# Layer 0 of a hybrid backbone: the context tokens' output projection and MLP made inside the attention stage

## The chip, the cores and the metric
One Trainium2 chip, one core of it. The metric is the device time of one launch in microseconds (us). The kernel before takes 4530.56 us, the median of three runs (4529.67 to 4532.49).

## The reference
Two layers act on 1024 latent tokens and 256 context tokens with 1024 channels. A layer normalises, projects into four head groups (gated DeltaNet, Hyena, HGRN2, differential attention), joins them, applies one output projection with a gated residual, then a squared-ReLU MLP with a gated residual. The last layer returns the latent tokens alone, so only layer 0 (and not layer 1) needs the context's output projection and MLP.

```python
def diff_attn_mixer(p_lat, p_ctx, ...):   # latent queries see context and latent keys
    ...                                   # context queries see context keys alone
# each layer, for both streams (the last layer: latent alone)
x = x + g1 * (concat(mixers) @ w_out)
h = modulate(x, ln2_w, shift2, scale2)
x = x + g2 * (square(relu(h @ mlp_w1)) @ mlp_w2)
```

## The kernel before, in words
Tokens lie along the free dimension: columns 0 to 1023 are latent, 1024 to 1279 context. Products of weights run three times, with operands split into a high and a low float32r part (`mm3`: wh·xh, wh·xl, wl·xh). `weight` loads a piece of a weight matrix of 128x512 into one of three `wraw` buffers through SP's DMA queue, ScalarE rounds it (`whi`), and GpSimd subtracts (`wlo`).

The instruction order is what the Python generators emit, then placed by a scheduler on each engine. `mix(lead, fill, ratio)` takes a lead generator and, after each step of weight w, as much of the fill as comes to ratio·w; what is left of the fill is drained at the end. `weave` does this between two fills. The attention stage (`mix(at[0], fill, RD[l])`) has `attn` as lead. Its fill (`rest`) is what is left of `hyena`, with the modulation products `mods` of this layer woven in, then `mods` of the next layer.

`attn` goes over four heads. Each has ten tiles of 128 queries: eight latent (1280 keys), then two context (256 keys). A tile is `scores` (the `psc` matmuls, a VectorE maximum, a ScalarE exponential, twice), `weights` (VectorE), `turn` (ten `ptr` transposes through PSUM, ScalarE copies), and per two tiles `values` (`pav`, `prb`); after a head, `norm` (`pss`). PSUM in this stage: two score tiles of three banks each, and two banks called `big`, which rotate among `ptr`, `pav`, `prb`, `pss`, hyena's and `mods`' tiles (`nbig` = 2, and `m` falls back on `big` when `nm` = 0).

`tail` comes after the attention stage, alone. It loads the mixers' outputs `o`, splits them, and goes over w_out (8 row blocks), then 8 MLP blocks of mlp_w1 (4 row blocks each) and mlp_w2 (8 each). With every weight piece loaded it makes three chunks of columns (512, 512, 256) in layer 0, two in layer 1, with five `big` banks. A chunk's 12 or 24 matmuls accumulate in one bank (`pt`); `residual` (VectorE, tile `tx`) or `hidden` (ScalarE Relu, VectorE square, split) empties it. Its last w_out pass, first mlp_w1 pass and last mlp_w2 pass go chunk by chunk and load their weights again.

Of the kernel before, what the change touches and what calls it, by code (L numbers as in the profile page):

```python
# [30 lines left out]
RC, RD, RM = [1.0, 1.0], [1.1, 0.8], [0.8, 0.8]  # L31
# [209 lines left out]
class K:  # L241


    def __init__(self, tc, ins, outs, dbg=None, upto=None):
        self.tc, self.nc, self.i, self.o = tc, tc.nc, ins, outs
        self.dbg, self.upto = dbg, upto
        self.done = set()
        self.pending = None

# [902 lines left out]
    def attn(self, l, qp):  # L1152
# [8 lines left out]
        def load(i, b):  # L1161

            out = ops[i, b] = []
            for j in range(2):
                for nm, n in (("q", 128 * NQ), ("k", T)):
                    t = pools[heads.index((i, b)) % 2].tile([128, T], F32R, tag=f"{nm}{j}", name=f"{nm}{j}")[:, :n]
                    c0 = 64 * b + 32 * j
                    nc.sync.dma_start(t.bitcast(F32), S["d" + nm, i][c0:c0 + 32, :, :n].rearrange("c r t -> (c r) t"))
                    out.append(t)

        pools = [qp]
        load(*heads[0])
# [21 lines left out]
        def scores(i, b, qi):  # L1194

            Q, Kt = ops[i, b][0::2], ops[i, b][1::2]
# [56 lines left out]
        def norm(i, b, oT):  # L1253
            tn = 64 * NQ
            o = S["o", 6 + i][64 * b:64 * b + 64, :128 * NQ].rearrange("e (q y t) -> y e q t", y=2, t=128)
            for a in range(0, tn, 320):
                e = min(tn, a + 320)
                sq = tp.tile([128, 320], F32, tag="sq", name="sq", bufs=1)[:, :e - a]
                r = tp.tile([128, 320], F32, tag="r", name="r", bufs=1)[:, :e - a]
                nc.scalar.activation(sq, oT[:, a:e], AF.Square)  # L1260
                p = self.m("pss")
                nc.tensor.matmul(p[:, :e - a], self.c["bones64"], sq, start=True, stop=True)
                self.rsqrt(r, p[:, :e - a], sq, 1.0 / 64, 64 * EPS)
                nc.vector.scalar_tensor_tensor(oT[:, a:e], oT[:, a:e], sw, r, ALU.mult, ALU.mult)
            for y in range(2):
                nc.gpsimd.dma_start(o[y], oT[64 * y:64 * y + 64, :tn].rearrange("e (q t) -> e q t", t=128))
# [3 lines left out]
        for h, (i, b) in enumerate(heads):  # L1270
            for qi in range(NQ):
                if qi == 2 and h + 1 < len(heads):
                    load(*heads[h + 1])
                cur = scores(i, b, qi)
# [3 lines left out]
                if qi == 0:  # L1278
                    old, oT = oT, tp.tile([128, 64 * NT], F32, tag="oT", name="oT")

                def todo(i=i, b=b, qi=qi, cur=cur, oT=oT):
# [8 lines left out]
                    if qi == NQ - 1:  # L1290
                        norm(i, b, oT)
# [280 lines left out]
    def tail(self, l, xp):  # L1572

        nc, tc, S = self.nc, self.tc, self.S
        full = l < DEPTH - 1
        toks = T if full else SEQ
        chunks = [(a, n) for a, n in CHUNKS if a < toks]
        M = self.Ms[l]
        nch = len(chunks)
        with ExitStack() as es:  # L1580
            hp = es.enter_context(tc.tile_pool(name=f"th{l}", bufs=1, side="right", reuse_waits="tile"))
            self.wp = es.enter_context(tc.tile_pool(name=f"tw{l}", bufs=2, side="right", reuse_waits="tile"))
            tp = es.enter_context(tc.tile_pool(name=f"tt{l}", bufs=4, reuse_waits="tile"))
            self.ps = self.fs = es.enter_context(tc.tile_pool(name=f"psT{l}", bufs=1, space=PSUM, reuse_waits="tile"))
            self.nbig, self.nm, self.nw, self.ww, self.lo_eng = 5, 3, 4, 512, nc.gpsimd

            def tmp(name, n):
                return tp.tile([128, 512], F32, tag="raw", name=name)[:, :n]

            def tiles(name):  # L1590

                return [[[hp.tile([128, n], F32R, tag=f"{y}{k}{a}", name=f"{name}{y}{k}")
                          for k in range(KT)] for a, n in chunks] for y in "hl"]
            oh, ol = tiles("o")
            for ks in (range(6), (6, 7)):
                for c, (a, n) in enumerate(chunks):
                    for k in ks:
                        raw = tmp("o", n)
                        nc.sync.dma_start(raw, S["o", k][:, a:a + n])
                        self.split(oh[c][k], ol[c][k], raw, lo_eng=nc.vector if k % 2 else nc.gpsimd)  # L1600
            x = []
            for k in range(KT):
                t = xp.tile([128, T], F32, tag=f"x{k}", name=f"tx{k}")
                nc.sync.dma_start(t[:, :toks], self.X[k][:, :toks])  # L1604
                x.append(t)
            rs = [xp.tile([128, n], F32, tag=f"r{a}", name=f"r{a}") for a, n in chunks]

            def product(wt, xh, xl, nk, done, cs):
                for c in cs:
                    a, n = chunks[c]  # L1610
                    p = self.big("pt")[:, :n]
                    for k in range(nk):
                        wh, wl = wt[k // 4]
                        sl = slice(128 * (k % 4), 128 * (k % 4) + 128)
                        self.mm3(p, wh[:, sl], wl[:, sl], xh[c][k], xl[c][k], k == 0, k == nk - 1)
                    done(p, c, a, n)

            def residual(m, G, norm=False, out=False):
                def done(p, c, a, n):
                    v = 0 if a < SEQ else 1  # L1620
                    xm = x[m][:, a:a + n]
                    nc.vector.scalar_tensor_tensor(xm, p, G[:, m, v:v + 1], xm, ALU.mult, ALU.add)  # L1622
                    if norm:
                        self.norm_sum(rs[c], xm, m, tmp("sq", n))
                        if m == KT - 1:
                            self.norm_factor(rs[c], rs[c], tmp("s4", n))
                    if out:
                        nc.sync.dma_start(out[m][:, a:a + n], xm)
                return done
            hh, hl = tiles("h")  # L1630
            for cs in ((0,), range(1, nch)):
                for m in range(KT):
                    product(self.weight(self.i["w_out"][l, m]), oh, ol, KT, residual(m, M["G1"], True), cs)
                for c in cs:
                    a, n = chunks[c]
                    v = 0 if a < SEQ else 1
                    for k in range(KT):
                        self.norm_apply(tmp("t", n), x[k][:, a:a + n], M["A2"][:, k, v:v + 1], M["B2"][:, k, v:v + 1], rs[c],
                                        hh[c][k], hl[c][k])
            if self.upto == "out":  # L1640
                return self.dump("x", lambda d: [nc.sync.dma_start(d[k], x[k]) for k in range(KT)]), rs
            if full:
                self.X = [self.dram(f"x{k}_{l}", [128, T]) for k in range(KT)]
                out = self.X
            else:
                out = self.o["yT"]
            with tc.tile_pool(name=f"tf{l}", bufs=1, reuse_waits="tile") as fp:
                for blk in range(8):
                    fh, fl = [[[fp.tile([128, n], F32R, tag=f"{y}{j}{a}", name=f"f{y}{j}") for j in range(4)]
                               for a, n in chunks] for y in "hl"]  # L1650

                    def hidden(j):
                        def done(p, c, a, n):
                            f = tmp("f", n)
                            nc.scalar.activation(f, p, AF.Relu)  # L1655
                            nc.vector.tensor_mul(f, f, f)  # L1656
                            self.split(fh[c][j], fl[c][j], f)
                        return done

                    for cs in (((0,), range(1, nch)) if blk == 0 else (range(nch),)):  # L1660
                        for j in range(4):
                            product(self.weight(self.i["mlp_w1"][l, 4 * blk + j]), hh, hl, KT, hidden(j), cs)
                    last = blk == 7
                    for cs in ([(c,) for c in range(nch)] if last else (range(nch),)):
                        for m in range(KT):
# [228 lines left out]
```

## Time and profile before

| what | value |
|---|---|
| median of three runs | 4530.56 us |
| the profiled execution, its own time | 4536.95 us |
| its span | 4535.1 us |
| mean granted TensorE clock | 0.932 of full speed |
| busy share of the span: TensorE, VectorE, ScalarE, GpSimd | 90%, 51%, 36%, 24% |

TensorE's share is high over the whole span, but it is an average over stages. In the page's 40 slices (113 us each) slices 11 to 14, in which layer 0's attention stage lies, show TensorE at 7 to 9 tenths with VectorE at 7 to 8, and slices 15 to 21 (layer 0's tail) TensorE at 9 tenths or more with VectorE at 2. A stage's end is set by the engine whose queue is fullest there and by who waits for whom.

### The profile page before, as it was taken

Reading aid. Unit: us, or ns where it says so; the run is one execution under the profiler, and the core shown is the slowest. Engines: PE = TensorE matmul, PEld = TensorE weight load, DVE = VectorE, ACT = ScalarE, POOL = GpSimd, SP = SyncE. Lnnn points to the kernel's source line nnn. Section 1 sums busy time; section 2 is a strip of 40 time slices with the busy share of each in tenths; the row PEclk is TensorE's granted clock in tenths of the full one; section 3 lists DMA queues with packets and bytes.
Section 4 is the critical chain, followed back from the end, with each engine's and each line's share of the span. In section 5 each row is a group of like instructions: output and inputs, shape, how many; then the busy total and the mean of one; then the engine's idle time right before and its main releaser. Section 6 shows DMA issues by size and latency. Waiting matters only on the chain. (4 is left out here: it accounts for less than half of the span.)

```text
span 4535.1 us, 81524 instructions
## 1 busy us (share of the span) xinstructions
PE 4064.8 (90%) x33312; PEld 3296.7 (73%) x33312; DVE 2330.6 (51%) x4579; ACT 1617.4 (36%) x3165; POOL 1075.7 (24%) x1101
## 2 busy tenths in 40 slices
PE   6998799887778799999999887999877789999999
PEld 3787677665555688888888766777655567888887
DVE  5856455766887452222222657556567875222222
ACT  4544512442445441111112554514324464212222
POOL 0234022000211343333333121121001215433333
PEclk8999899987889899999999998899877889999999
DMA  5335743335323421111112336534342233111112
GB/s 180 103 116 159 189 126 123 103 122 186 119 82 136 147 70 38 40 38 40 38 38 70 98 89 170 177 109 141 123 169 104 68 130 126 61 49 49 49 49 89
DMA packets 387434, 466.48 MB, mean 103 GB/s; under 512 B 137683, under 2 KB 246355, under 8 KB 385140
## 3 DMA queue, kind: packets, MB, share of 16 engines
q1 hardware_dynamic: 385236, 456.28, 31.2%
q8 instruction: 263, 4.31, 0.4%
q0 software_dynamic: 1824, 4.98, 0.4%
q14 instruction: 111, 0.91, 0.1%
HBM read 341.71 MB, written 119.44 MB: 102 GB/s over the span
## 5 line engine op out<-in xcount | busy, mean ns | idle before, releaser
L255 POOL TENSOR_TENSOR wlo<-wraw,whi 128x512 fp32r<-128x512 f32 x360 | 478.8, 1336 | 737.7 <-ACT whi L254 735.5
L254 ACT CAST whi<-wraw 128x512 fp32r<-128x512 f32 (+1 forms) x480 | 296.4, 620 | 910.5 <-PE pt L260 752.4
L1622 DVE SCALAR_TENSOR_TENSOR tx<-pt,mod,tx 128x512 f32<-128x512 f32 (+1 forms) x360 | 250.9, 697 | 589.9 <-PE pt L261 588.9
L261 PE MATMUL pt<-hh,wlo 128*128 128x512 f32 (+1 forms) x1280 | 471.7, 368 | 2.8 <-POOL wlo L255 2.8
L260 PE MATMUL pt<-fl,whi 128*128 128x512 f32 (+1 forms) x1280 | 472.5, 369 | 0.0
L260 PE MATMUL pt<-hl,whi 128*128 128x512 f32 (+1 forms) x1280 | 472.4, 369 | 0.0
L259 PE MATMUL pt<-hh,whi 128*128 128x512 f32 (+1 forms) x1280 | 471.7, 369 | 0.4 <-ACT f L1655 0.4
L259 PE MATMUL pt<-fh,whi 128*128 128x512 f32 (+1 forms) x1280 | 471.7, 369 | 0.0
L261 PE MATMUL pt<-fh,wlo 128*128 128x512 f32 (+1 forms) x1280 | 471.7, 369 | 0.0
L1656 DVE TENSOR_TENSOR f<-f 128x512 f32<-128x512 f32 (+1 forms) x160 | 149.5, 936 | 622.7 <-ACT f L1655 616.9
L259 PE MATMUL pproj<-hh,whi 128*128 128x512 f32 (+1 forms) x960 | 372.4, 388 | 10.9 <-ACT u L500 10.7
L260 PE MATMUL pproj<-hl,whi 128*128 128x512 f32 (+1 forms) x960 | 362.7, 378 | 0.0
L261 PE MATMUL pproj<-hh,wlo 128*128 128x512 f32 (+1 forms) x960 | 360.2, 375 | 0.0
L255 POOL TENSOR_TENSOR fl<-f,fh 128x512 fp32r<-128x512 f32 (+1 forms) x160 | 191.5, 1198 | 390.3 <-ACT fh L254 390.3
L261 PEld LDWEIGHTS pt<-hh,wlo 128*128 128x128 f32 x1280 | 241.4, 189 | 44.2 <-POOL wlo L255 4.0
L259 PEld LDWEIGHTS pt<-hh,whi 128*128 128x128 f32 x1280 | 241.5, 189 | 40.9 <-ACT f L1655 0.8
L259 PEld LDWEIGHTS pt<-fh,whi 128*128 128x128 f32 x1280 | 241.5, 189 | 40.9 <-ACT whi L254 0.2
L261 PEld LDWEIGHTS pt<-fh,wlo 128*128 128x128 f32 x1280 | 241.3, 189 | 40.6 <-issue 0.5
L260 PEld LDWEIGHTS pt<-fl,whi 128*128 128x128 f32 x1280 | 241.5, 189 | 40.3 <-POOL fl L255 0.3
L260 PEld LDWEIGHTS pt<-hl,whi 128*128 128x128 f32 x1280 | 241.5, 189 | 40.1 <-issue 0.2
L529 PE MATMUL pproj<-whi,hh 128*128 128x256 f32 (+2 forms) x624 | 193.0, 311 | 35.9 <-ACT whi L254 21.7
L259 PEld LDWEIGHTS pproj<-hh,whi 128*128 128x128 f32 x960 | 187.1, 195 | 51.3 <-ACT u L500 12.9
(376 smaller groups left out, 8292.6 us busy)
## 6 DMA issues: line engine op xcount, KB each, us to landing
wraw<-mlp_w SPq DMA_DIRECT2D x296, 256.0 KB
modw<-mod_w SPq DMA_DIRECT2D x80, 512.0 KB
wraw<-w_cm SPq DMA_DIRECT2D x88, 256.0 KB
wraw<-w_out SPq DMA_DIRECT2D x64, 256.0 KB
kv<-kvd SPq DMA_DIRECT2D x40, 256.0 KB
k<-dk SPq DMA_DIRECT2D x16, 640.0 KB
modw<-mod_w SPq DMA_DIRECT2D x4, 2048.0 KB
ksl<-X SPq DMA_DIRECT2D x16, 512.0 KB
```

The source lines that it names most:

```text
L254: (hi_eng or nc.scalar.copy)(hi, src)
L255: (lo_eng or nc.gpsimd).tensor_tensor(lo, src, hi.bitcast(F32), ALU.subtract)
L259: nc.tensor.matmul(ps, wh, xh, start=start, stop=False)
L260: nc.tensor.matmul(ps, wh, xl, start=False, stop=False)
L261: nc.tensor.matmul(ps, wl, xh, start=False, stop=stop)
L529: nc.tensor.matmul(p[:, :w - c0], hh[k][:, sl], wh[:, b + c0:b + w], start=first, stop=False)
L1622: nc.vector.scalar_tensor_tensor(xm, p, G[:, m, v:v + 1], xm, ALU.mult, ALU.add)
L1656: nc.vector.tensor_mul(f, f, f)
```

## The change
In layer 0, `attn` takes the context queries of all four heads first (two tiles each, with their own loads of q and k), then the latent queries of all four. `tail` becomes a generator that takes its chunks, its pools and its output as arguments. `tail_context` runs it for the context's 256 columns; it follows hyena in the attention stage's fill, with the next layer's `mods` woven in at 0.3, and the stage's ratio `RD[0]` goes from 1.1 to 1.6. The context's result goes to DRAM (`Xn`, and the norm's factor `Rn`). The tail after the attention stage makes the two latent chunks, and takes the context's columns of x and its factor back from DRAM. Layer 1 has the same work as before (its `norm` goes by 256 columns in place of 320).

```diff
-RC, RD, RM = [1.0, 1.0], [1.1, 0.8], [0.8, 0.8]
+RC, RD, RM = [1.0, 1.0], [1.6, 0.8], [0.8, 0.8]
...
     def attn(self, l, qp):
-        NQ = NT if full else NLT
+        seq = [(i, b, range(*r)) for r in ([(NLT, NT)] if full else []) + [(0, NLT)] for i in range(2) for b in range(2)]
...
-                for nm, n in (("q", 128 * NQ), ("k", T)):
+                for nm, r in (("q", slice(128 * qs[0], 128 * qs[-1] + 128)), ("k", slice(0 if lat else SEQ, T))):
...
-            for a in range(0, tn, 320):
-                e = min(tn, a + 320)
+            for a in range(t0, tn, 256):
+                e = min(tn, a + 256)
...
-        for h, (i, b) in enumerate(heads):
-            for qi in range(NQ):
-                if qi == 2 and h + 1 < len(heads):
-                    load(*heads[h + 1])
-                cur = scores(i, b, qi)
+        for s, (i, b, qs) in enumerate(seq):
+            for qi in qs:
+                if qi - qs[0] == (2 if len(qs) > 2 else 0) and s + 1 < len(seq):
+                    load(s + 1)
+                cur = scores(s, qi)
...
-    def tail(self, l, xp):
+    def tail(self, l, xp, es, chunks, side, out, store=None):
...
+        yield x, rs
...
             def product(wt, xh, xl, nk, done, cs):
...
+                yield n / 512 * nk / KT
...
+        if store is not None:
+            nc.sync.dma_start(store, rs[0])
+
+    def tail_context(self, l):
+        assert self.ctx_out
+        with ExitStack() as es:
+            xp = es.enter_context(self.tc.tile_pool(name=f"txc{l}", bufs=1, side="right", reuse_waits="tile"))
+            g = self.tail(l, xp, es, CHUNKS[2:], "right", self.Xn, self.Rn)
+            next(g)
+            yield from g
...
                             yield from weave(self.hyena(l), m2, RM[l])
                             if full:
-                                yield from self.mods(l + 1, range(16), mp)
+                                self.Xn = [self.dram(f"x{k}_{l}", [128, T]) for k in range(KT)]
+                                self.Rn = self.dram(f"r_{l}", [128, CTX])
+                                yield from weave(self.tail_context(l), self.mods(l + 1, range(16), mp), 0.3)
...
-                xs, rs1 = self.tail(l, xp)
+                    g = self.tail(l, xp, ts, LCHUNKS, "left", self.Xn if full else self.o["yT"])
+                    xs, rs1 = next(g)
+                    if full:
+                        for k in range(KT):
+                            nc.sync.dma_start(xs[k][:, SEQ:], self.Xn[k][:, SEQ:])
+                        nc.sync.dma_start(rs1[2], self.Rn)
+                    run(g)
```

TensorE, between two latent tiles of the attention stage after hyena has ended (`ptr` transposes, `psc` scores, `pmod` modulation, `pt` tail products). Before:

```order
L1230 MATMUL ptr<-c_ident,p_15100 128x128 x10
L368 MATMUL pmod<-modw,cst 32x128 x8
L354 MATMUL pmodT<-c_sel,modr 128x2 x4
L1230 MATMUL ptr<-c_ident,p_15186 128x128 x8
L1208 MATMUL psc<-k_14524,q_14522 128x512
L1230 MATMUL ptr<-c_ident,p_15186 128x128 x2
L1208 MATMUL psc<-k_14524,q_14522 128x512
L1242 MATMUL pav<-wT,vt 64x128 x20
L1248 MATMUL prb<-c_ident,rb 128x128
```

And with the change, where 48 `pt` matmuls follow the last row shown:

```order
L369 MATMUL pmod<-modw,cst 32x128 x8
L1234 MATMUL ptr<-c_ident,p_15099 128x128 x4
L1212 MATMUL psc<-k_14354,q_14352 128x256
L1234 MATMUL ptr<-c_ident,p_15099 128x128 x6
L1246 MATMUL pav<-wT,vt 64x128 x20
L1252 MATMUL prb<-c_ident,rb 128x128
L1212 MATMUL psc<-k_14358,q_14356 128x512 x2
L1212 MATMUL psc<-k_14358,q_14356 128x256
L1212 MATMUL psc<-k_14354,q_14352 128x512
L260 MATMUL pt<-hh_14705,whi 128x256
```

Groups of 24 to 96 context products now stand between the tiles' own matmuls; all 1728 lie between the first score and the tail, 1296 of them ahead of the last head's `pss`, 432 behind it.

SP's DMA queue, where the context's part ends and the tail after it begins (`tx_14...` is the context's x, `tx_19...` the x of the tail, `x_0_...` DRAM):

```order
L1637 DMA x_0_14625<-tx_14700 128x256
L1873 DMA tx_19250<-x_0_14624 128x256
L1637 DMA x_0_14626<-tx_14702 128x256
L1873 DMA tx_19252<-x_0_14625 128x256
L1873 DMA tx_19254<-x_0_14626 128x256
L1671 DMA r_14627<-r_14704 128x256
L271 DMA wraw<-w_out 128x512 x3
L1874 DMA r_19258<-r_14627 128x256
L1606 DMA o<-o_0_123 128x512
```

The tail's first weights stand behind the context's last stores and their loads back.

## Rows read from the trace of the kernel before

**Rows 1.** Busy time by stretch: us from span's start, length, each engine, clock, DMA share, GB/s.

```profile
core 0: us, PE busy (x) PEld busy (x) DVE busy (x) ACT busy (x) POOL busy (x), PEclk, DMA share, GB/s
1125.00:1385.00 260.00, 186.41 (x1314) 144.99 (x1314) 213.37 (x275) 107.86 (x202) 47.34 (x52) 0.83 0.28 99
1385.00:1497.00 112.00, 90.22 (x1005) 65.17 (x1003) 78.34 (x136) 65.90 (x134) 11.39 (x22) 0.92 0.43 147
1125.00:1497.00 372.00, 276.63 (x2316) 210.16 (x2316) 291.71 (x410) 173.76 (x335) 58.73 (x74) 0.86 0.32 114
1497.00:1600.00 103.00, 85.75 (x369) 68.00 (x369) 45.35 (x59) 41.77 (x74) 45.79 (x36) 0.88 0.45 151
1497.00:2528.00 1031.00, 1009.14 (x5197) 862.28 (x5196) 314.91 (x427) 268.41 (x487) 361.38 (x290) 0.99 0.19 61
3727.00:4535.00 808.00, 792.60 (x3460) 651.96 (x3460) 226.07 (x270) 212.61 (x354) 321.11 (x246) 0.99 0.21 70
```

**Rows 2.** Timeline of TensorE: start, us, instruction; in layer 0's tail, then in attention.

```profile
1700.72 0.28 PE L259 MATMUL pt<-fh,whi 128*128 128x256 f32 x1
1700.84 0.28 PE L260 MATMUL pt<-fl,whi 128*128 128x256 f32 x1
1700.96 0.28 PE L261 MATMUL pt<-fh,wlo 128*128 128x256 f32 x1
...
1702.04 0.40 PE L260 MATMUL pt<-fl,whi 128*128 128x512 f32 x1
1702.27 0.39 PE L261 MATMUL pt<-fh,wlo 128*128 128x512 f32 x1
...
1452.82 0.71 PE L1230 MATMUL ptr<-c_ident,p 128*128 128x128 f32 x5
```

**Rows 3.** Groups by form in layer 0's tail (1500:2530): count, busy us, mean ns, idle before.

```profile
L255 POOL TENSOR_TENSOR wlo<-wraw,whi 128x512 fp32r<-128x512 f32 x180 | 241.3, 1349 | 411.1 <-ACT whi L254 410.2 <-issue 0.3
L254 ACT CAST whi<-wraw 128x512 fp32r<-128x512 f32 x180 | 111.0, 618 | 394.7 <-PE pt L260 380.5 <-DMA wraw<-w_out 6.2 <-issue 5.6
L261 PE MATMUL pt<-fh,wlo 128*128 128x256 f32 x256 | 72.9, 285 | 0.0
L1656 DVE TENSOR_TENSOR f<-f 128x256 f32<-128x256 f32 x32 | 37.9, 1185 | 74.6 <-ACT f L1655 72.6 <-POOL fl L255 2.1
L1622 DVE SCALAR_TENSOR_TENSOR tx<-pt,mod,tx 128x256 f32<-128x256 f32 x72 | 34.7, 483 | 46.0 <-PE pt L261 46.0
L255 POOL TENSOR_TENSOR fl<-f,fh 128x256 fp32r<-128x256 f32 x32 | 23.5, 736 | 0.0
```

**Rows 4.** Groups by form, attention after hyena's end (1385:1497).

```profile
L1209 DVE TENSOR_REDUCE mx<-psc 128x1 f32<-128x1280 f32 x23 | 34.2, 1485 | 3.9 <-PE psc L1208 3.8
L1210 ACT ACTIVATE p<-psc,mx 128x1280 f32<-128x1280 f32 x23 | 30.6, 1331 | 14.2 <-DVE mx L1209 11.3 <-DVE mod L355 1.5 <-DVE sm L1217 1.2
L1230 PE MATMUL ptr<-c_ident,p 128*128 128x128 f32 x144 | 25.2, 308 | 4.7 <-DVE modr L376 1.7 <-ACT wT L1232 1.4 <-DVE mod L355 0.8
L1220 DVE SCALAR_TENSOR_TENSOR p<-p,sm,p 128x1280 f32<-128x1280 f32 x12 | 18.6, 1549 | 0.4
L1232 ACT COPY wT<-ptr 128x512 f32<-128x512 f32 x28 | 15.5, 588 | 18.3 <-PE ptr L1230 18.3
L1209 DVE TENSOR_REDUCE mx<-psc 128x1 f32<-128x256 f32 x8 | 3.4, 420 | 0.9 <-PE psc L1208 0.8
```

**Rows 5.** Groups by form, attention with hyena beside it (1125:1385).

```profile
L1230 PE MATMUL ptr<-c_ident,p 128*128 128x128 f32 x192 | 33.0, 307 | 13.9 <-DVE sm L1217 5.2 <-DVE u L1563 2.2 <-DVE p L1220 2.2
L1557 PE MATMUL py<-bil,X 128*128 128x256 f32 x128 | 39.0, 472 | 16.2 <-DVE X L1546 11.4 <-issue 4.7
```

**Rows 6.** Who waited for whom in 1385:1497: us in total, times, longest.

```profile
PEld psc L1208 <- ACT p L1210: 13.1, 13, 4.2
...
PEld ptr L1230 <- ACT wT L1232: 4.5, 12, 1.1
...
PEld pmod L368 <- ACT wT L1232: 3.9, 9, 1.0
```

More of the change, by code (lines that the diff above doesn't have):

```diff
@@ L1569, in hyena @@
         es.close()
-    def tail(self, l, xp):
+    def tail(self, l, xp, es, chunks, side, out, store=None):
         nc, tc, S = self.nc, self.tc, self.S
-        full = l < DEPTH - 1
-        toks = T if full else SEQ
-        chunks = [(a, n) for a, n in CHUNKS if a < toks]
+        t0, t1 = chunks[0][0], sum(chunks[-1])
+        wide = chunks[0][1]
         M = self.Ms[l]
         nch = len(chunks)
-        with ExitStack() as es:
[L1581 to L1665, printed above, removed]
-                            product(self.weight(self.i["mlp_w2"][l, blk, m], 512, 1), fh, fl, 4,
-                                    residual(m, M["G2"], last and full, last and out), cs)
-        return x, rs
@@ new lines, in tail, with tmp, tiles @@
+        pool = lambda name, bufs, side: es.enter_context(
+            tc.tile_pool(name=f"{name}{side[0]}{l}", bufs=bufs, side=side, reuse_waits="tile"))
+        full = l < DEPTH - 1
+        hp = pool("th", 1, "right")
+        self.wp = pool("tw", 2, "right")
+        self.nw, self.ww, self.lo_eng = 4, 512, nc.gpsimd
+        tp = pool("tt", 4, side)
+        def tmp(name, n):
+            return tp.tile([128, wide], F32, tag="raw", name=name)[:, :n]
+        def tiles(name):
+            return [[[hp.tile([128, n], F32R, tag=f"{y}{k}{a}", name=f"{name}{y}{k}")
+                      for k in range(KT)] for a, n in chunks] for y in "hl"]
@@ new lines, in tail @@
+        oh, ol = tiles("o")
+        for ks in (range(6), (6, 7)):
+            for c, (a, n) in enumerate(chunks):
+                for k in ks:
+                    raw = tmp("o", n)
+                    nc.sync.dma_start(raw, S["o", k][:, a:a + n])
+                    self.split(oh[c][k], ol[c][k], raw, lo_eng=nc.vector if k % 2 else nc.gpsimd)
+        x = []
+        for k in range(KT):
+            t = xp.tile([128, T if side == "left" else t1 - t0], F32, tag=f"x{k}", name=f"tx{k}")
+            nc.sync.dma_start(t[:, :t1 - t0], self.X[k][:, t0:t1])
+            x.append(t)
@@ new lines, in tail, with product @@
+        rs = [xp.tile([128, n], F32, tag=f"r{a}", name=f"r{a}") for a, n in (CHUNKS if full and side == "left" else chunks)]
+        yield x, rs
+        def product(wt, xh, xl, nk, done, cs):
+            for c in cs:
+                a, n = chunks[c]
+                p = self.big("pt")[:, :n]
+                for k in range(nk):
+                    wh, wl = wt[k // 4]
+                    sl = slice(128 * (k % 4), 128 * (k % 4) + 128)
+                    self.mm3(p, wh[:, sl], wl[:, sl], xh[c][k], xl[c][k], k == 0, k == nk - 1)
+                done(p, c, a, n)
+                yield n / 512 * nk / KT
@@ new lines, in tail @@
+        hh, hl = tiles("h")
+        for cs in ((0,), range(1, nch)):
+            for m in range(KT if cs else 0):
+                yield from product(self.weight(self.i["w_out"][l, m]), oh, ol, KT, residual(m, M["G1"], True), cs)
+            for c in cs:
+                a, n = chunks[c]
+                v = 0 if a < SEQ else 1
+                for k in range(KT):
+                    self.norm_apply(tmp("t", n), x[k][:, a - t0:a - t0 + n], M["A2"][:, k, v:v + 1], M["B2"][:, k, v:v + 1],
+                                    rs[c], hh[c][k], hl[c][k])
```

81 lines of the change are left out of this document (60 added, 21 removed).

## The prediction
> **What bounds the kernel now.** I read the busy times by stretch first, then TensorE's timeline, then the groups by form, then the waits. The stretches [rows 1] show two stages that differ in kind. Layer 0's tail (1497 to 2528, 1031 us) is TensorE's: busy 1009 of 1031 us at a granted clock of 0.99, VectorE busy 315. The attention stage ahead of it (1125 to 1497, 372 us) is nobody's: VectorE 292 us, TensorE 277 us at a clock of 0.86, GpSimd 59 us. It has two parts. Until 1385 hyena runs beside the tiles and VectorE is busy 213 of 260 us (82%). From 1385 on only the modulation products are left as fill, VectorE falls to 70%, and the stage is paced by the tile's own chain score, maximum, exponential, weights, transposes: the scores wait for the exponential that frees their bank, 13.1 us [rows 6].
>
> The change moves the context's share of the tail into that slack. So the sum has three questions: what the tail loses, how much the attention stage grows, and what the seam costs.
>
> **The tail loses 223 us.** In its steady state a matmul of 256 columns starts 0.12 us after the one before, one of 512 columns 0.23 us [rows 2]. The context has 256 of the 256-column form in each of six groups of the MLP (one of them is in [rows 3]) and 192 in w_out, 1728 in all: 1728 x 0.12 = 207 us. Layer 1's tail is already what layer 0's becomes, two chunks of 512 with the same weights: 808 us against 1031 [rows 1], 223 less. The 16 us beyond the matmuls are the third chunk's splits and evacuations around the passes. I take 223.
>
> **What the attention stage gets.** By the order the 1728 matmuls stand between latent tiles, 1296 ahead of the last head's norm and 432 behind it. They bring their own weights: the context can't share the pieces that the tail loads, so 16 + 64 + 64 = 144 pieces of 128x512 are loaded, rounded and subtracted once more (the eight that the tail saves, its third pass over the last mlp_w2 block, are in the 223). Prices [rows 3]: GpSimd 1.35 us a piece, 194 us, and 0.74 us for each of 32 hidden tiles, 24 us; ScalarE 0.62 us a piece, 89 us; VectorE 72 residuals at 0.48 us, 35 us, and 32 squares at 1.19 us, 38 us. 144 x 256 KB is 38 MB of DMA; the queues are busy 0.32 of the stage [rows 1], so I cost it at nothing. Its cover is the prefetch through three raw buffers; if it fails, each piece shows as a wait of `whi` for a DMA. SP's queue is in order: q and k of the next head stand behind weight loads, but are asked for at a head's third tile, five tiles ahead, which covers them.
>
> I cut the new stage in three.
>
> *(a) Up to the first context product.* By the order this holds all of hyena, the 8 context tiles and 12 latent tiles. Before, the stretch up to 1385 held hyena, about 18.4 latent and 4 context tiles (192 transposes, ten and two a tile [rows 5]). A latent tile costs VectorE 2 x 1.485 + 1.549 = 4.5 us, a context tile some 1.3 us (estimate: three operations of 0.42) [rows 4]. VectorE: 213 - 6.4 x 4.5 + 4 x 1.3 = 189 us; at the same 82% that is 230 us. The first heads now have two tiles each, so the q and k loads for them and for the first latent head come closer together: 4 us. I take 234, with 222 (VectorE at 85%, loads hidden) and 245 (77%) as bounds.
>
> *(b) 20 latent tiles with 1296 context matmuls.* Without the products: before, from 1385 on, 13.6 latent and 4 context tiles (144 transposes [rows 4]) took 112 us; with 2 us for a context tile (1.3 at 70%) a latent tile takes 7.6 us, 20 of them 153 us. The products are 1296 x 0.12 = 156 us. If nothing overlaps: 309 us. If everything does, TensorE's own work remains: 156 plus per tile 1.2 us of scores, 1.1 us of transposes at 0.11 us each [rows 2], and at most 1.1 us of values (estimate, at the transposes' pace), 68 us, and some 6 us of modulation: 230 us. The others lie below: GpSimd 108 pieces and 24 hidden tiles 163 us, ScalarE 20 x 4.4 + 108 x 0.62 + 18 = 173 us, VectorE 90 + 26 + 27 and small ones, 150 us. The nearest row for four engines sharing one order is the hyena stretch, in which the fullest was busy 82%: 223/0.82 is 272. I take 270, with 230 and 309 as bounds, and more than 309 if banks stall (below).
>
> *(c) The 432 left over.* Nothing else runs: TensorE 52 us, GpSimd 36 x 1.35 + 9 x 0.74 = 55 us; these two run in step. I take 57 (55 to 65).
>
> Sum 234 + 270 + 57 = 561 us, 189 more than the 372.
>
> **The seam.** Before, the tail's first weights and most of its first inputs were there when attention ended, and it waited for the last head: 86 busy of its first 103 us [rows 1]. Now SP's queue has the context's eight stores, their loads back and the norm factor ahead of `wraw<-w_out`, so the first split waits for the context's last residual, its norm and a DMA or two. 6 us (0 to 12), queued behind it all of the tail. It replaces the wait for the last head's output, which is out of the way by then.
>
> **Sum:** -223 + 189 + 6 = -28 us. The profiled execution took 4536.95 us, so 4509 in its terms; it lies 6.4 us above the median of the runs, so 4503 for them.
>
> **Rivals.**
> 1. *Full overlap*: the products fill TensorE's idle time and lift its clock, so tile and product cost TensorE's own work alone. For it: the clock is 0.83 to 0.92 in this stage and 0.99 in the tail [rows 1], and no engine but TensorE would be over 75% busy in (b). Against it: one order on each engine, two banks. Price: (b) 235, (c) 55, seam 3: 234 + 235 + 55 = 524, +152 + 3 - 223 = -68 us, 4463.
> 2. *The two banks* (the other side). Every product holds one of the two `big` banks for its 12 or 24 matmuls, 1.4 or 2.9 us, and until VectorE or ScalarE has emptied it; the emptying queues behind a 1.49 us maximum or a 1.33 us exponential [rows 4]. Transposes and values use the same two in turn, so after each group of products TensorE waits. If that costs 1.3 us a tile on top of no overlap, (b) is 309 + 26 = 335, (c) 60, seam 8: 629, +257 + 8 - 223 = +42 us, 4573. It decides from (b) = 298 us on, 14.9 us a tile, where the gain is used up. Against it: today the waits of transposes and modulation for a ScalarE copy are only 4.5 + 3.9 of 112 us [rows 6], though those tenants hold a bank far shorter than a product will. The Trainium skill (Perfetto Trace Analysis, "Optimizing Tensor Performance" and "Matmul Optimizations") says that independent matmul groups should rotate through different banks so that emptying one overlaps the next, and that all eight should be in use; here six are tied to scores. By that rule the time is this rival's; the trace of before supports it only by those small waits.
> 3. *It doesn't move*: the products pile up behind the last tile. The order fixes 432 of 1728 there, so at most that part is a mere move; its time is in (c).
>
> **How the numbers follow.** About 9 us (0.2%) is what a measurement of this kernel can tell from no change. Chances: forecast 0.58, full overlap 0.2, two banks 0.2, something unseen 0.02. (b) above 307 us means slower by over 9 us: 0.2; (b) between 289 and 307 means within it: 0.13; the rest, 0.67, is faster. The range takes in full overlap, somewhat better (4455), and most of the bank rival (4565); best and worst ends of all terms together, 4443 and 4575, are left outside. The forecast's own range is 4475 to 4530.
>
> **What the profile after would show.** Right: the last tail some 808 to 815 us long with no 256-column `pt`; the attention stage 530 to 590 us, TensorE busy over 80% in (b) at a clock of 0.95 or more; GpSimd 160 to 200 us busy there. Rival 1: (b) near 12 us a latent tile. Rival 2: (b) at 15 us or more, with TensorE's `ptr` and `pt` waiting for `wT`, `tx` or `f`. The prediction would also be wrong if `whi` waits for DMA or `prb` for a row sum that GpSimd queues behind `wlo`, or if (a) takes more than 245 us because the first heads wait for q and k.

## The result and the profile after

The changed kernel takes 4588.28 us (median of four runs, 4584.7 to 4594.47) against 4530.52 us before: 1.013 times the time, 95% interval 1.0118 to 1.0141, 58 us slower. The forecast was 28 us faster, in a range that ended at 4565. The profiled execution has a span of 4592.7 us; before it was 4535.1.

Busy time by stretch of the changed kernel, with the columns of [rows 1]. In order: the stage's first 75 us, the stage up to hyena's last product, up to the first context product, the part with products and tiles, the leftover, the seam, layer 0's tail, layer 1's tail.

```profile
1125.00:1200.00 75.00, 40.55 (x233) 29.97 (x232) 43.52 (x97) 17.10 (x54) 11.92 (x15) 0.61 0.54 187
1125.00:1358.00 233.00, 150.29 (x968) 115.48 (x967) 172.51 (x261) 65.70 (x147) 45.48 (x49) 0.75 0.34 118
1125.00:1411.00 286.00, 190.75 (x1365) 145.31 (x1364) 211.53 (x319) 95.27 (x205) 57.14 (x64) 0.76 0.38 132
1411.00:1716.00 305.00, 264.52 (x2232) 236.76 (x2231) 170.25 (x229) 172.09 (x336) 172.18 (x154) 0.95 0.39 124
1716.00:1788.00 72.00, 63.28 (x503) 59.46 (x501) 25.81 (x42) 28.55 (x58) 48.28 (x42) 0.91 0.68 219
1788.00:1797.00 9.00, 2.38 (x11) 2.23 (x12) 3.24 (x9) 4.40 (x9) 2.61 (x3) 0.62 0.56 174
1797.00:2594.00 797.00, 791.04 (x3462) 650.43 (x3460) 237.61 (x278) 223.62 (x371) 323.42 (x246) 1.00 0.21 67
3785.00:4590.00 805.00, 794.09 (x3460) 652.31 (x3460) 227.42 (x268) 211.90 (x353) 321.82 (x246) 0.99 0.22 70
```

All stretches start at 1125 us, as in [rows 1]. But the stage's first score does not: it starts at 1125.52 us in the kernel before (first fence: start, length in us) and at 1139.76 us with the change (second).

```profile
1125.52 1.86 PE L1208 MATMUL psc<-k,q 128*128 128x512 f32 x4 [0.67 <-ACT fg L1690]
```

```profile
1139.76 0.79 PE L1212 MATMUL psc<-k,q 128*128 128x256 f32 x2 [0.68 <-ACT fg L1702]
```

So 14 of the 286 us up to the first context product lie ahead of the stage. Five of them had gathered 256 us earlier (the first `pfin` after 850 us starts at 874.4 us for 869.1), in work that the change leaves as it was; nine came after that, at the end of the stage before.

Against the forecast: (a) 286 us for 234; (b) 305 for 270; (c) 72 for 57; seam 9 for 6. From 1125 to the tail's first matmul it is 671 us where it had been 374, 297 more. The tail lost 228, counted from its first product to its last (1025 us before, 797.5 after; forecast 223). That leaves 69 us lost at layer 0's end; what follows was 12 us shorter. So the tail is as forecast, and the stage is 104 us longer than forecast: half of that in (a).

The rows that answer to [rows 3, 4, 5]: first the transposes up to hyena's last product (1125:1358) and from there to the first context product (1358:1411), then groups of the part with products (1411:1716).

```profile
L1234 PE MATMUL ptr<-c_ident,p 128*128 128x128 f32 x86 | 14.6, 292 | 4.8 <-DVE u L1569 1.8 <-DVE p L1224 1.2 <-ACT wT L1236 1.0
L1234 PE MATMUL ptr<-c_ident,p 128*128 128x128 f32 x50 | 9.9, 340 | 3.1 <-DVE modr L377 1.9 <-DVE u L1569 0.7 <-DVE mod L356 0.3
...
L256 POOL TENSOR_TENSOR wlo<-wraw,whi 128x512 fp32r<-128x512 f32 x108 | 147.0, 1368 | 104.8 <-ACT whi L255 90.1 <-PE pt L261 10.1 <-PE pt L262 1.2
L255 ACT CAST whi<-wraw 128x512 fp32r<-128x512 f32 x108 | 66.3, 619 | 77.2 <-PE pt L261 51.8 <-DMA wraw<-mlp_w 12.8 <-issue 5.0
L1213 DVE TENSOR_REDUCE mx<-psc 128x1 f32<-128x1280 f32 x35 | 51.6, 1482 | 12.5 <-PE psc L1212 12.4
L1658 DVE TENSOR_TENSOR f<-f 128x256 f32<-128x256 f32 x24 | 25.1, 1046 | 38.4 <-ACT f L1657 35.3 <-POOL wlo L256 3.1
```

86 transposes are 16 of the eight context tiles and 70 of seven latent tiles: only seven stand beside hyena, the other five of (a) run behind it. Before, 18 did. Durations of single instructions are near those of before. What changed is who waits: beside hyena, TensorE's wait for hyena's own `X` is 30.6 us with the change (first fence: us in total, times, longest) and 11.4 before (second).

```profile
PE py L1563 <- DVE X L1552: 30.6, 4, 13.9
```

```profile
PE py L1557 <- DVE X L1546: 11.4, 3, 4.8
```

TensorE's waits in the part with products (us in total, times, longest):

```profile
PE ptr L1234 <- ACT f L1657: 8.5, 5, 2.9
PE psc L1212 <- ACT p L1214: 8.4, 3, 4.2
PE pt L260 <- ACT wT L1236: 3.7, 6, 1.5
PE ptr L1234 <- ACT wT L1236: 3.4, 5, 1.1
```

Transposes wait for a bank that a product held (`f`), products for one that a transpose held (`wT`): the signs of rival 2, each small.

### The profile page after: what moved, and what is told of

It reads as the page before. It is cut to its first block, busy times and chain, and to the rows that moved or that the text cites. A ratio compares the mean times of both kernels' runs of the same rounds, so it can differ in the third digit from the quotient of the medians.

```text
span 4592.7 us, 82357 instructions
## 1 busy us (share of the span) xinstructions
PE 4084.5 (89%) x33320; PEld 3308.9 (72%) x33320; DVE 2364.8 (51%) x4591; ACT 1699.3 (37%) x3317; POOL 1261.8 (27%) x1245
## 5 line engine op out<-in xcount | busy, mean ns | idle before, releaser
L256 POOL TENSOR_TENSOR wlo<-wraw,whi 128x512 fp32r<-128x512 f32 x496 | 658.7, 1332 | 764.1 <-ACT whi L255 747.4
L255 ACT CAST whi<-wraw 128x512 fp32r<-128x512 f32 (+1 forms) x616 | 380.3, 620 | 1003.9 <-PE pt L261 806.1
L1658 DVE TENSOR_TENSOR f<-f 128x512 f32<-128x512 f32 (+1 forms) x160 | 165.7, 1037 | 617.4 <-ACT f L1657 603.6
L262 PEld LDWEIGHTS pt<-fh,wlo 128*128 128x128 f32 x1280 | 244.8, 191 | 40.1 <-issue 0.2
```

The source lines that it names most:

```text
L255: (hi_eng or nc.scalar.copy)(hi, src)
L256: (lo_eng or nc.gpsimd).tensor_tensor(lo, src, hi.bitcast(F32), ALU.subtract)
L262: nc.tensor.matmul(ps, wl, xh, start=False, stop=stop)
```

## The experiments

Seventeen kernels ran, each against the kernel before on the same chip. In the table, the first column is the start of the stage's first score (in e15 and e16 it waits some 8 us for its `k`). Stretches run between starts of matmuls in the trace: from 1125 to hyena's last `py`, to the first context `pt`, to the last `pss`, to the last context `pt`, to the tail's first `pt`. Latent tiles are ten transposes each. "Each" is the price of a product: in the part with products after taking off 7.7 us a tile (with the new order and no products, 18 tiles behind hyena took 138 us); that split is an estimate, since products and tiles share TensorE.

| run | first score at | to hyena's end (latent tiles) | to first product (tiles) | with products (tiles, products, each) | leftover (products, each) | seam | 1125 to tail | median |
|---|---|---|---|---|---|---|---|---|
| the change | 1140 | 233 (7) | 53 (5) | 304 (20, 1296, 0.116) | 72 (432, 0.168) | 9 | 671 | 4588.3 |
| e2_rd11 | 1139 | 259 (14) | 55 (7) | 141 (11, 480, 0.117) | 207 (1248, 0.166) | 10 | 672 | 4590.6 |
| e3_weight | 1132 | 259 (13) | 42 (4) | 228 (15, 924, 0.122) | 137 (804, 0.170) | 10 | 675 | 4595.2 |
| e4_bank3 | 1132 | 221 (7) | 51 (5) | 286 (20, 1304, 0.101) | 71 (424, 0.167) | 10 | 638 | 4662.6 |
| e5_supply | 1136 | 226 (7) | 54 (5) | 296 (20, 1296, 0.109) | 66 (432, 0.153) | 8 | 649 | 4576.3 |
| e6_rd11_supply | 1138 | 255 (14) | 55 (7) | 142 (11, 480, 0.119) | 191 (1248, 0.153) | 9 | 652 | 4572.6 |
| e7_bank_supply | 1130 | 218 (7) | 47 (5) | 285 (20, 1304, 0.101) | 64 (424, 0.151) | 9 | 623 | 4560.4 |
| e9_fl_dve | 1138 | 232 (7) | 52 (5) | 305 (20, 1296, 0.116) | 71 (432, 0.164) | 10 | 669 | 4598.3 |
| e10_dense | 1132 | 251 (14) | 55 (7) | 346 (11, 1728, 0.151) | none | 14 | 666 | 4602.6 |
| e11_dense_bank_supply | 1135 | 274 (14) | 67 (7) | 312 (11, 1728, 0.132) | none | 8 | 662 | 4589.0 |
| e12_two | 1141 | 231 (7) | 52 (5) | 267 (20, 864, 0.131) | 66 (288, 0.228) | 17 | 634 | 4555.1 (one run) |
| e15_best | 1146 | 257 (10) | 54 (6) | 218 (16, 903, 0.105) | 122 (825, 0.148) | 9 | 661 | 4582.3 |
| e16_preload | 1138 | 226 (7) | 52 (5) | 305 (20, 1296, 0.116) | 72 (432, 0.166) | 9 | 663 | 4592.2 |
| e18_best | 1133 | 224 (7) | 51 (5) | 288 (20, 1304, 0.103) | 65 (424, 0.153) | 10 | 637 | 4560.4 |

Medians do not follow the column before them to the microsecond. The first score's start differs between profiles, and with the same work it takes 1987 to 2011 us from the tail's last product to the program's end (e4 apart; see the last section).

**The order alone, and the ratio.** The first kernel keeps the new order of queries and drops the rest; the next two set the ratio, or the weight of a context tile.

```diff
# e1_order: ratio 1.1, tail with CHUNKS, no reload of x, and
-  yield from weave(self.tail_context(l), self.mods(l + 1, range(16), mp), 0.3)
+  yield from self.mods(l + 1, range(16), mp)
# e2_rd11
-RC, RD, RM = [1.0, 1.0], [1.6, 0.8], [0.8, 0.8]
+RC, RD, RM = [1.0, 1.0], [1.1, 0.8], [0.8, 0.8]
# e3_weight: in attn, each yield times wt
+  wt = 1.0 if qs[0] < NLT else 0.3
```

> The order of queries alone: context heads first, fill ratio 1.1 as before, no context tail in the fill, the tail with its three chunks. Theory A (the eight short context tiles, put in a row, leave hyena uncovered): the attention stage grows from 372 us by 15 to 35 us, VectorE is busy under 65% in its first 75 us, and the time is 4545 to 4565 us. Rival (the short tiles cost nothing, what lengthened the first part is the ratio 1.6 alone): stage within 8 us of 372, time within 10 us of 4530.

> The whole change with the fill ratio back at 1.1. Theory A (hyena uncovered at ratio 1.6): more latent tiles stand beside hyena, so its part takes about as long as now (283 us) with some 6 latent tiles more in it; those tiles leave the part with the products, whose leftover behind the last head grows: about 635 us from stage start to the tail against 668, time near 4555 us. Rival (the first part takes as long as its work on VectorE needs, whatever the ratio): the first part grows by 7.6 us a tile moved into it and the leftover comes on top, time 4590 to 4610 us.

> The whole change at ratio 1.6, but a context tile draws 0.3 of the fill that a latent tile draws, so that hyena spreads over some 6 more latent tiles. Theory A: hyena's part keeps its 283 us with 17 to 18 latent tiles in it instead of 12, 14 tiles with products follow (about 215 us), then a leftover of some 800 products (about 115 us): near 630 us to the tail against 668, time near 4550 us. Rival (the first part pays for each tile): time 4585 to 4600 us.

The order alone: 4552.24 us, 1.0048 times before (1.0031 to 1.0065). Its stage is 16 us longer (390 from 1125 to the tail, against 374): the first score is 7 us late (1132.8 us), and from there to the tail it is 382 us for 374. VectorE is less busy at the start:

```profile
1125.00:1200.00 75.00, 39.32 (x225) 29.26 (x225) 44.27 (x99) 21.42 (x67) 13.85 (x20) 0.66 0.56 199
1125.00:1376.00 251.00, 174.24 (x1210) 134.34 (x1210) 201.07 (x290) 96.44 (x204) 48.07 (x58) 0.81 0.34 118
1376.00:1514.00 138.00, 109.82 (x1128) 80.89 (x1126) 94.07 (x145) 82.09 (x154) 12.36 (x24) 0.89 0.38 124
```

The kernel before had VectorE busy 61.73 us in those 75 us, at a clock of 0.82:

```profile
1125.00:1200.00 75.00, 52.75 (x382) 40.80 (x383) 61.73 (x80) 36.42 (x66) 12.48 (x14) 0.82 0.41 148
```

Counted from each kernel's own first score, VectorE's 75 us hold 62.23 us before and 45.95 with the order alone.

A tile's price beside hyena is read from first score to hyena's last `py`: 243 us (e1) and 244 (e2) with 14 latent tiles, 218 with seven (the change), so 3.5 to 3.7 us a tile; behind hyena it costs 7.7. The ratio of 1.6 thus moved seven tiles at half price to where they cost 4 us more each: some 28 us. Theory A holds for that, and the rival's 7.6 us a tile does not. Theory A's forecast of a gain at ratio 1.1 does not hold either: e2 and e3 got those tiles back beside hyena, yet the time to the tail stayed at 672 and 675 us, because more products fell behind the last head, where each costs 0.17 us in place of 0.12. Their times (4590.6, 4595.2) lie in the rival's range, for another reason than the rival's.

**Banks and weight buffers.**

```diff
# e4_bank3: a third bank in turn for transposes, values, modulation, products
+  self.turn3 = (self.turn3 + 1) % 3
+  if self.turn3 == 2:
+      return self.ps.tile([128, 512], F32, tag="b3", name=name, bufs=1)
# paid for by one score tile of five banks for both halves
-  A = self.ps.tile([128, 1536], F32, tag="s", name="psc", bufs=2)[:, :n]
+  A = self.sc[:, T * j:T * j + n]
# e5_supply, for the context's pieces: wraw, whi, wlo
-  self.nw = 4                       # and wraw with bufs=3
+  self.nw = 6                       # and wraw with bufs=6
# e6: e5 at ratio 1.1; e7: e5 and e4's bank in layer 0 alone
# e9_fl_dve
-  self.split(fh[c][j], fl[c][j], f)
+  self.split(fh[c][j], fl[c][j], f, lo_eng=nc.vector if side == "right" else None)
```

> The whole change with a third rotating PSUM bank for transposes, values, modulation and products; the two score tiles share five banks instead of six. Theory B (two banks: TensorE waits before transposes and products until a copy, a residual or a Relu has emptied one, 21.6 and 19 us of start-to-start loss in the 305 us with products): that loss falls by half or more, the part takes 280 us or less, time 4555 to 4570 us. Rival (the order alone, products and tiles in turn on TensorE, whatever the banks): within 5 us of 305, time within 8 us of 4588.

> The whole change with more buffers for the context's weight pieces: six raw ones instead of three, six rounded and six subtracted ones instead of four. Theory C (a piece that is loaded, rounded and subtracted through few buffers sets the pace where nothing else runs: 0.168 us a product behind the last head against 0.12 of TensorE's pitch): the leftover of 432 products takes 55 to 60 us instead of 72, the time is 4565 to 4578 us. Rival D (the context's single chunk leaves nothing to cover the way from one block's Relu to the next block's products, whatever the buffers): leftover 68 to 74 us, time within 8 us of 4588.

> Ratio 1.1 and the larger weight buffers together. At ratio 1.1 some 1248 products are left over at 0.166 us each. Theory C: they fall to 0.125 to 0.135, 40 to 50 us less, time 4540 to 4552 us. Rival D: within 10 us of 4590.

> The whole change, the larger weight buffers, and the third bank in layer 0 alone (layer 1 keeps two score tiles of three banks and two big banks). Theory B, by the run with three banks in both layers, whose layer 0 was 33 us shorter up to the tail: 33 us less than the run with the larger buffers alone, layer 1 as with the change, so 4535 to 4560 us. Rival (that gain was of that run alone, or the buffers give it already): within 10 us of the run with the larger buffers alone.

> The whole change, with the context's hidden tiles subtracted on VectorE instead of GpSimd, so that fl no longer stands behind the weights' wlo in GpSimd's queue. Theory D (the way Relu, square, rounding, subtraction between a block's two products is what the leftover waits for): leftover 60 to 66 us instead of 72, the part with products up to 5 us shorter, time 4572 to 4582 us. Rival C (weights' buffers): leftover within 2 us of 72, time within 6 us of 4588.

The third bank shortens the part with products from 304 to 286 us, in the run without larger buffers, and from 296 to 285 with them (the granted clock there was 0.95 in the change, 0.96 in e5, 0.98 in e4 and e7, so not all of it need be waits for banks); the transposes' wait for `f` is gone from the head of TensorE's list (run with bank and buffers, 1390:1675):

```profile
PE psc L1225 <- ACT p L1227: 6.1, 9, 2.7
PE pmean L412 <- DVE r L407: 3.4, 1, 3.4
PE pav L1259 <- ACT wT L1249: 3.2, 2, 3.0
PE pt L263 <- POOL fl L258: 3.1, 4, 1.0
```

So theory B is part of the cause: at most 11 to 18 us. The forecast of 280 us or less, and of a whole run of 4555 to 4570, was missed, the latter because the bank's price falls due in layer 1, where no products run beside the tiles: from its first transposes to its last `pss` that stage is 365 us long with the third bank (first fence) and 271 in the change itself (second).

```profile
3477.00:3842.00 365.00, 257.95 (x1836) 197.91 (x1834) 219.88 (x290) 151.51 (x275) 40.04 (x53) 0.75 0.21 68
```

```profile
3512.00:3783.00 271.00, 218.72 (x1825) 168.78 (x1825) 219.28 (x288) 149.85 (x273) 38.40 (x53) 0.86 0.27 92
```

The buffers take 0.168 us of a leftover product to 0.153, not to the 0.125 to 0.135 that theory C asked for; e5's leftover of 66 us and e6's time of 4572.57 us lie between theory C and rival D. What ScalarE waits for changes as it should: in e2's leftover (1580:1787) `whi` waits for loads and for its own buffers, in e5's (1702:1767) the loads are gone from the list.

```profile
ACT whi L255 <- PE pt L261: 46.6, 35, 3.6
ACT whi L255 <- DMA wraw<-mlp_w: 40.5, 33, 3.1
```

```profile
ACT whi L256 <- PE pt L262: 18.4, 17, 3.0
DVE tx L1632 <- PE pt L263: 15.3, 13, 2.4
```

Moving `fl` to VectorE changed neither part by over 2 us: theory D, as put for that run, falls. Bank and buffers together (e7) give 4560.44 us, 1.0059 (1.004 to 1.0079): better than the change, slower than before, and just past the upper end of theory B's 4535 to 4560.

**Density, length and the bank by itself.**

```diff
# e10_dense (ratio 1.1); e11: the same with e7's bank and buffers
+  for w in weave(self.tail_context(l), self.mods(l + 1, range(16), mp), 0.3):
+      yield w * 0.27
# e12_two: mm3 for the context
-  nc.tensor.matmul(ps, wl, xh, start=False, stop=stop)
# e13_before_bank: the kernel before, e4's bank in layer 0
```

> The whole change at ratio 1.1 beside hyena, but the steps of the context tail (with the modulation woven in) count 0.27 of what they did, so that nearly all 1728 products stand between the 11 latent tiles that are left behind hyena. Theory A with prices from the runs so far (hyena with 14 latent tiles 259 us, 7 tiles 55 us, 11 tiles of 7.7 us and 1728 products of 0.117 us, seam 9 us): 610 us to the tail against 668, time 4525 to 4540 us. Rival D (a product costs what it does behind the last head, 0.168 us, wherever tiles are too few to cover its chain): 675 us, time 4585 to 4600 us.

> The same with the larger weight buffers and the third bank in layer 0. By the prices of the run with both (0.101 us a product, hyena's part 12 us shorter): 570 to 580 us to the tail, time 4495 to 4515 us, below the kernel before. Rival D: 0.15 us a product, 635 us to the tail, time 4550 to 4565 us.

> The whole change, with the context's third matmul of each product (wl by xh) left out: 1152 context matmuls instead of 1728, all loads, roundings and subtractions as they were. Theory E (in the part with products TensorE's time simply adds to the tiles' own): 432 of the 1296 go, that part is 50 us shorter (254 us). Rival B (each swap of TensorE between tiles and products waits for a bank, whatever the products' length): 20 us or less shorter. The leftover: if TensorE paced it, 72 falls to 50 us; if the weights' pieces pace it, 62 us or more stay.

> The kernel before with the third bank in layer 0's attention stage alone. Theory F (a score tile waits there for both exponentials of the pair, which products cover but nothing else does): the stage is 50 us or more longer than 372. Rival (the bank helps the stage as it is): 350 to 365 us.

Packing all products between 11 tiles costs 0.151 us each, nearer to rival D's 0.168 than to theory A's 0.117, and the time is 4602.6 us, just above rival D's range. That the price depends on how much else stands between two products of the context's single chain fits these runs, but no run shows it by itself. Bank and buffers bring it to 0.132 (e11), but there hyena's part is 274 us for 251, with 14 tiles beside it and the score halves coupled; its 662 us to the tail and 4589 us miss both forecasts.

With a third of the matmuls left out, the part with products is 37 us shorter for 432 fewer, 0.086 us each: between theory E (50) and rival B (20). TensorE's own time is the larger part of what a product costs there. The granted clock in that part was 0.91 (first row) for the change's 0.95; at the same clock more would have been saved. The leftover stays at 66 us, with TensorE busy 48.64 of them (second row): at that length it is not TensorE that paces it.

```profile
1411.00:1678.00 267.00, 218.60 (x1787) 187.29 (x1779) 172.36 (x229) 170.76 (x338) 175.72 (x154) 0.91 0.45 141
1678.00:1744.00 66.00, 48.64 (x354) 42.78 (x355) 23.51 (x43) 27.72 (x56) 47.86 (x42) 0.91 0.72 222
```

The third bank by itself, in the kernel before (4599.21 us, one run), makes the stage 446 us long for 372, up to the last `pss`; 6 of the 74 us lie ahead of its first score (1131.2 us). TensorE's largest wait, scores for exponentials, is 70.3 us there (first fence) and 40.1 before (second):

```profile
PE psc L1220 <- ACT p L1222: 70.3, 32, 4.5
```

```profile
PE psc L1208 <- ACT p L1210: 40.1, 24, 6.5
```

So theory F holds: coupling the halves costs a stage without products 68 to 74 us, 30 of them in this one wait, and is covered where products run.

**The order's 16 us.**

```diff
# e14: first latent head's q, k ahead of the stage, the context's at its start; e16: the same in the whole change
-  load(0)
+  load(4 if full else 0)
# e17: the context's four heads ahead of the stage, the first latent head at its start
-  load(0)
+  for s in range(4 if full else 1):
+      load(s)
# e15: e14's loads, bank, buffers, ratio 1.35; e18: e17's loads, bank, buffers, ratio 1.6
```

> The order of queries alone at ratio 1.1, but with the loads moved: the first latent head's q and k are asked for ahead of the stage, as in the kernel before, and the four context heads' share one set of tiles, all asked for at the stage's start. Theory G (the order costs its 16 us because q and k of the first latent head, 2.3 MB, stand in SP's queue just ahead of hyena's next 1 MB loads, and TensorE waits for both): stage 375 to 382 us instead of 390, VectorE busy 52 us or more of the first 75 instead of 44, time 4532 to 4542 us. Theory A (eight short tiles do not cover hyena, wherever the loads stand): stage within 5 us of 390, time 4547 to 4557 us.

> The whole change with all that helped so far: the moved loads, the larger weight buffers, the third bank in layer 0, and a ratio of 1.35, between the two tried. By the prices so far: 4560 us of the run with bank and buffers, less 10 (loads), less 5 to 10 (some 4 tiles more beside hyena at 2.5 us in place of 7.7, against products that move behind the last head at 0.05 us more each): 4540 to 4548 us, still above the kernel before. Rival (the loads bring nothing and the ratio evens out): 4555 to 4568 us.

> The whole change, with the moved loads alone. Theory G: hyena's part 10 us shorter than its 233, time 4575 to 4582 us. Theory A: within 6 us of 4588.

> The order of queries alone at ratio 1.1, with q and k of all four context heads asked for ahead of the stage, and those of the first latent head at its start (in the run with the loads moved the other way, the first context tile waited 9.6 us for its own k). Theory G (the loads): no wait of TensorE for q, k or u over 3 us in the stage's first 75 us, the stage 375 to 382 us, time 4532 to 4542 us. Theory A (short tiles): those waits are gone too, yet VectorE is busy under 48 of the first 75 us, the stage 385 us or more, time 4545 to 4556 us.

> The whole change at 1.6 with the larger weight buffers, the third bank in layer 0, and the loads as in the run beside it. Theory G: 10 us less than the run with bank and buffers alone (4560 us), near 4550 us. Theory A: within 8 us of 4560. By neither does it reach the kernel before.

TensorE's waits in the first 75 us with the order alone (first fence), with the loads moved one way (e14, next), and the other way (e17, last):

```profile
PE psc L1212 <- ACT p L1214: 14.5, 6, 10.7
PE psc L1212 <- DMA k<-dk: 6.3, 1, 6.3
...
PE put L1499 <- DMA u<-yv: 4.7, 1, 4.7
```

```profile
PE psc L1225 <- DMA k<-dk: 10.2, 2, 9.6
```

```profile
PE psc L1226 <- ACT p L1228: 20.1, 7, 10.7
...
PE put L1513 <- DMA u<-yv: 3.6, 1, 3.6
```

e14 only moved the wait to another load and gained nothing (4550.98 us). e17 has no wait for k and takes 4539.85 us, 1.0014 (1.0004 to 1.0024), in theory G's range, and its stage 383 us for 390: the loads are some 7 us of the order's 16. Most of that lies ahead of the stage, since the first score comes at 1127.5 us for e1's 1132.8; from there to the tail it is 381 us for 382. Theory G's range of 375 to 382 was missed by one, and a wait for `u` of 3.6 us is left. VectorE is still busy only 47.88 of the first 75 us, as theory A said. What it waits for is seen in e17's timeline (start, us, instruction, idle before; L1513 and L1348 are hyena's):

```profile
1150.51 0.42 DVE L1227 TENSOR_REDUCE mx<-psc 128x1 f32<-128x256 f32 x1 [1.16 <-PE psc L1226]
...
1154.11 2.93 PE L1513 MATMUL put<-c_ident,u 128*128 128x128 f32 x12 [3.63 <-DMA u<-yv]
...
1158.65 0.29 DVE L598 SCALAR_TENSOR_TENSOR sq<-pss,sq 128x128 f32<-128x128 f32 x1 [7.71 <-ACT sq L597]
...
1161.69 6.48 PE L1348 MATMUL pF<-ut,bfl 128*128 128x256 f32 x24
```

Hyena's `put` waits for its load at the head of TensorE's queue, the head's `pss` and the tile's transposes stand behind it, and VectorE, done with the short tile's maximum in 0.42 us (1.49 for a latent one [rows 4]), idles 7.7 us. In the whole change the same load orders bring little: e16 4592.18 us and e18 4560.44 us, no better than without; e15, at ratio 1.35, is worse than e7 and outside both of its forecasts (4582.29 us).

No version of the change beat the kernel before.

## Why the prediction was wrong, point by point

- **The tail, -223.** Right: 797 us, 228 less.
- **(a), 234 us, took 286.** The step that failed is "VectorE: 213 - 6.4 x 4.5 + 4 x 1.3 = 189 us; at the same 82% that is 230 us". It takes 12 latent tiles as if all stood beside hyena; seven did, and five ran behind it. 14 of the 286 us lie ahead of the first score. From there it is 271 us (first fence), with VectorE busy 201.01 us, 74%; the second fence is the kernel before, from its first score to hyena's last product, with 82%.

```profile
1139.76:1411.06 271.30, 182.03 (x1308) 138.72 (x1308) 201.01 (x291) 92.85 (x198) 57.14 (x64) 0.77 0.39 133
```

```profile
1125.50:1384.00 258.50, 185.41 (x1307) 144.10 (x1308) 212.37 (x274) 107.21 (x200) 47.34 (x52) 0.83 0.28 100
```

The share was no property of the stretch: with seven tiles beside hyena TensorE waited 30.6 us for hyena's own `X`, with 18 (before) 11.4 and with 14 (e1) 5.9. So taking a tile away saved 3.5 to 3.7 us and not 4.5/0.82 = 5.5. By that price 12 tiles beside hyena would have taken some 236 us (an estimate: e1's 243 less two tiles), near the forecast; the five behind it took 53 us, where beside it they would have cost 18. These 35 us and the 14 ahead of the first score are nearly all of the 52. Five of the 14 are a difference between runs that the change did not make. The other nine hang on the loads of q and k: with the context's loads ahead of the stage (e17, e18) nothing is lost there, in the other runs with the new order 2 to 9 us. The prediction had named and priced that term at 4, inside the stage.
- **(b), 270 us, took 305.** It is inside the bounds of 230 and 309, at the upper one. The share assumed for the fullest engine, 82%, was not what failed: TensorE was busy 87%. What failed is its work: "156 plus per tile 1.2 us of scores, 1.1 us of transposes at 0.11 us each [rows 2], and at most 1.1 us of values (estimate, at the transposes' pace), 68 us, and some 6 us of modulation: 230 us". TensorE was busy 264.52 us. By the timeline, each matmul counted up to the next one's start or its own end, the products take 171 of them, the tiles 84 and the rest 10. 115 of the 1296 products start the next one 0.21 us later and not 0.12, which is 11 us; the transposes take 0.13 us each. And the products did not fill TensorE's idle time: it is 40 us with 20 tiles here, and 28 of 138 us with e1's 18 tiles and no products. So next to nothing ran beside the products, as in the bound "If nothing overlaps: 309 us". Rival 2's banks are at most 11 to 18 us of it, weight buffers 8 in e5 and nothing in e6, where fewer products stand there. The Trainium skill's rule on rotating banks (Perfetto Trace Analysis, "Optimizing Tensor Performance") fits the part with products (304 to 286 us). In the stage without them, where the bank had to be taken from the scores, the time grew (446 for 372). How that order could be made to overlap was not shown by any run.
- **(c), 57 us, took 72.** The step that failed: "Nothing else runs: TensorE 52 us, GpSimd 36 x 1.35 + 9 x 0.74 = 55 us; these two run in step." TensorE was busy 63.28 us: 4 of it are modulation that runs in between, and 56 of the 432 products start the next one 0.21 us later and not 0.12 (granted clock 0.91), 5 us. It idles 9 us more. Something other than TensorE holds the leftover at 66 us (e12, with a third of the matmuls gone). Raw buffers and loads are a part (6 us by e5); the rest was not settled, and not `fl`'s place in GpSimd's queue (e9).
- **The seam, 6 us, took 9.** Inside its bounds.
- **Layer 1, 0, gave back 12.** It was not in the sum, and it is luck, as far as the runs show: the same work took 1987 to 2011 us in the profiles, 2011 in that of the kernel before and 1999 in that of the change.
- **The rivals.** The slower side was given 0.2 and 4573 us, by banks alone. Its price for (b) was 335 us; (b) came out at 305, above its break-even of 298 but short of its price. (a) alone, for which no rival was written, lost 52 us, more than the forecast gain of 28; (b), (c) and the seam lost 53 together. Full overlap (235 for (b)) was as far off as could be.

## What to carry to other kernels

A busy share read from a stretch belongs to the mix of work in it: when one of two interleaved chains is thinned out, price the removal by what the remaining chain then leaves idle, not by the share. Work put "into slack" between the steps of another chain can cost its full time; 1728 matmuls that cost 228 us in a well-filled tail cost 281 us here (671 less the order's 390; 275 if each is counted from its first score). A bank gained for one tenant is a bank taken from another, and the exchange may pay in one stage and cost five times as much in the next.

## What the runs showed of the hardware that was not expected

Layer 1 before its attention runs the same instructions in both kernels, yet the stretch between the same two matmuls took 177 us before (first fence) and 163 after (second), at a granted clock of 0.87 and 0.95 (2.4 GHz is 1.0), with TensorE busy 155 and 142 us. What decides between the two was not found; it covers the 12 us that layer 1 gave back.

```profile
3126.00:3303.00 177.00, 155.38 (x2699) 116.73 (x2698) 112.43 (x328) 70.22 (x148) 6.68 (x10) 0.87 0.36 119
```

```profile
3193.00:3356.00 163.00, 141.66 (x2697) 106.47 (x2697) 112.30 (x327) 70.11 (x148) 6.77 (x10) 0.95 0.39 129
```

The clock also fell where the stage was thinned: in the 75 us from the first score it was 0.67 with the change (first fence) and 0.82 before (second), while TensorE was busy 45.08 and 53.25 us of them. Hyena's `put` transposes there took 417 ns in place of 284 (medians). What the lower clock adds to (a) was not separated.

```profile
1139.76:1214.76 75.00, 45.08 (x261) 33.60 (x262) 43.96 (x89) 18.80 (x59) 12.55 (x18) 0.67 0.56 191
```

```profile
1125.50:1200.50 75.00, 53.25 (x383) 41.22 (x384) 62.23 (x80) 35.92 (x65) 12.48 (x14) 0.82 0.41 148
```
